# Head blocks 512 columns wide in a seven-phase transformer kernel, with MLA's mask, constants and two weight splits moved

## The chip, the cores and the metric

The kernel runs on one core of a Trainium2 chip. The time is device microseconds of one execution, and what counts is the median of several. TensorE (PE) multiplies matrices, VectorE (DVE) and ScalarE (ACT) work on elements, GpSimd (POOL) does a few small powers here, and SyncE (SP) issues the DMAs. Matmuls write to PSUM, eight banks of 512 fp32 values a partition; the other engines take the results from there to SBUF.

## The reference

Everything is fp32, for 256 positions and a model width of 1024. Two blocks run one after the other; in the first, each of two layers is a mixer and an MLP, each closed by a layer norm on the residual sum.

```python
# first block: layer 0 mixes by a short convolution, layer 1 by multi-head latent attention (MLA)
x = layer_norm(ALPHA * x + mixer(x))
x = layer_norm(ALPHA * x + square(relu(x @ w1)) @ w2)        # w1 1024 x 4096
# second block
x = x + 0.5 * ((silu(h @ w_gate) * (h @ w_up)) @ w_down)     # h = rms_norm(x), w_gate 1024 x 2816
x = x + hybrid(rms_norm(x))                                  # w_in to z, xbc, dt, q, k, v; SSD and attention; w_out
x = x + 0.5 * swiglu(rms_norm(x)); return rms_norm(x)
# inside MLA, 8 heads, chunks of 64 positions
ckv, kpe = split(x @ w_dkv, 256);  ckv = rms_norm(ckv, g_kv);  kpe = rope(kpe)
cq = rms_norm(x @ w_dq, g_q);  q = cq @ w_uq                 # 128 + 64 (rope) a head
k, v = ckv @ w_uk, ckv @ w_uv
s = (q_nope @ k.T + q_pe @ kpe.T) * scale
p = softmax(where(k_chunk <= q_chunk, s, -inf));  y = (p @ v) @ w_o
```

## The kernel before

Seven phases follow each other: sc (short convolution), mlp0, mla, mlp1, ffn1, hyb and ffn2. TensorE keeps fp32 accuracy by splitting each operand into a high and a low part: a product is three matmuls, high times high, high times low weight, low activation times high weight (`mmx`, L176 to L178).

All weights go through one stream. A list, the plan, names the tiles in the order in which they are used, mostly 512 KB each (128 partitions of 1024 values). SP's queue loads a tile into one of four raw buffers; ScalarE casts it to the high part (L156), VectorE subtracts that from the raw tile for the low part (L157); eleven such pairs can be in SBUF. `take(n, ahead)` hands out the next n pairs and starts the splits of those behind them, `rel` gives pairs back. SP's instructions run in the order in which the program writes them. On the other engines a scheduler sets the order, with a higher priority for the end of a phase (`fin`).

The positions are two halves of 128, hh = 0 and 1. A phase ends with the accumulators of half 0, whose norm then runs on VectorE beside the matmuls of half 1. The next phase begins with "head" blocks: `xblock` holds a 128 x 128 piece of the transposed activations in the array and streams 256 weight columns, 8 pieces of the contraction, for half 0; `flush_norm` then transposes the normalised rows of half 1, and the same weights are used for that half. mlp0 and mlp1 have four such blocks in front (`m`), ffn1 and ffn2 two of the gate and two of the up weights (`pg`, `pu`), hyb four of v and z and later two more of z (`vz`). The weights of these blocks lie in HBM as 4 KB a partition for 256 columns and four contraction pieces. What follows a head streams 512 columns, of activations in the wide blocks (`wd`) and of weights in the output blocks (`acc`).

MLA has no such head; its first matmuls are `pkv` (w_dkv, 320 columns) and `pq` (w_dq, 384 columns), again for half 0 and then half 1. `chain_kv` normalises a half's ckv (`ch`) and turns its kpe (`rope`, results in `kp`); both are transposed later (`tp<-ident,ch` and `tp<-ident,kp`). g_q, g_kv and the rope's table are loaded into three work buffers at the start of MLA. Behind the two halves stands the line that starts the splits of w_uv, w_uk and w_uq:

```python
wuv, wuk, wuq = self.take(2, 0), self.take(2, 0), self.take(6, 0)
```

`scores` writes four heads, or two for the 256 keys of half 1, into a bank `sc`: a matmul with k, one with kpe, and a third that adds the mask as the product of a row of ones for the first 64 queries and a row of a large negative number for the last 64 keys (`mr`, bf16). `soft` takes the maximum, the exponentials (ScalarE, one for each head) and the sum, and multiplies by its reciprocal (`pp<-pp,rc`). The eight heads go in two groups of four; between them stand a v projection, the k projections and the q projections of the second group, whose results VectorE copies out (`qT`, L776).

Of the kernel before, what the change touches and what calls it, by code (L numbers as in the profile page):

```python
# [16 lines left out]
P = 128  # L17
D = 1024
S = 256
# [15 lines left out]
WORK_BUFS = 37  # L35
# [51 lines left out]
class Core:  # L87
# [48 lines left out]

    def dma_ahead(self):
        while self.n_dma < len(self.plan) and self.n_dma < self.n_split + RAW_BUFS:
            src, nk, nn = self.plan[self.n_dma]
            r = self.rawp.tile([P, SUB], F32, tag="raw", name="raw")  # L140
            self.nc.sync.dma_start(out=r[:, :nk * nn].rearrange("p (k n) -> p k n", k=nk), in_=src)
            self.raw[self.n_dma] = r
            self.n_dma += 1

    def pump(self, n=99):

        nc = self.nc
        self.dma_ahead()
        while n > 0 and self.n_split < len(self.plan) and self.n_split < self.n_rel + W_BUFS:
            i = self.n_split  # L150
            _, nk, nn = self.plan[i]
# [6 lines left out]
            self.wt[i] = (h[:, :m].rearrange("p (k n) -> p k n", k=nk), l[:, :m].rearrange("p (k n) -> p k n", k=nk))  # L158
            self.n_split += 1
            self.dma_ahead()  # L160
            n -= 1
# [123 lines left out]
    def layer_norm(self, hh, acc, g, b):  # L285
# [119 lines left out]
    def sc(self, fin):  # L405
# [4 lines left out]
        for b in range(4):  # L410
# [22 lines left out]
            if b == 0:  # L433
                self.constants()
        self.tail(self.new_acc(), [(vT, k) for k in range(8)], True, fin, 4)

    def constants(self):
# [18 lines left out]
        nc.vector.tensor_scalar(out=self.ones, in0=self.tri, scalar1=0.0, scalar2=1.0, op0=ALU.mult, op1=ALU.add)  # L456

# [63 lines left out]
    def plan_mlp(self, i):  # L521
        w1, w2 = self.t["ff_w1"][2 * i:2 * i + 2], self.t["ff_w2"][i]
        f = {"a": lambda j: self.wi(w1, j * S), "b": lambda j: [self.wap(w2, 2 * j + k, 1, 0, D) for k in range(2)]}
        nb = D_FF // S
        o = ([("a", j) for j in range(self.HEAD)] + self.mlp_order(nb, self.HEAD, self.TAIL)
             + [("b", j) for j in range(nb - self.TAIL, nb)])
        return [x for c, j in o for x in f[c](j)]
# [28 lines left out]
    def mlp(self, fin):  # L556
# [4 lines left out]
        for hh in range(2):  # L561
            for j in range(self.HEAD):
# [4 lines left out]
                self.xblock(ps[:, (j % 2) * S:(j % 2 + 1) * S], xT, hh, ws[j])  # L567
# [28 lines left out]
    def plan_ffn(self, i):  # L596
# [4 lines left out]
        o = ([("a", j) for j in range(self.HEAD2)] + self.mlp_order(nb, self.HEAD2, self.TAIL2)  # L601
             + [("b", j) for j in range(nb - self.TAIL2, nb)])
        return [x for c, j in o for x in f[c](j)]

    def ffn(self, fin):
# [60 lines left out]
    def mla(self, fin):  # L666
        nc, xT = self.nc, self.xT
        gq, gkv = self.work(name="gq")[:, :384], self.work(name="gkv")[:, :256]
        nc.sync.dma_start(out=gq, in_=self.t["mla_g_q"][0].partition_broadcast(P))
        nc.sync.dma_start(out=gkv, in_=self.t["mla_g_kv"][0].partition_broadcast(P))  # L670
        rt = self.work(name="rope")[:, :256].rearrange("p (h c r) -> p h c r", h=2, c=2)
# [3 lines left out]
        mr = self.const.tile([1, 3, S], BF16, tag="mr", name="mr")  # L675
        nc.vector.memset(mr, 0.0)
        nc.vector.memset(mr[:, 0, 0:64], 1.0)
        nc.vector.memset(mr[:, 1, 64:128], NEG)
        nc.vector.memset(mr[:, 2, 192:256], NEG)
# [49 lines left out]
        wuv, wuk, wuq = self.take(2, 0), self.take(2, 0), self.take(6, 0)  # L729
# [50 lines left out]
        def scores(hh, heads):  # L780
            nk = P * (hh + 1)
            ps = self.ps("sc")
            for i, h in enumerate(heads):
# [5 lines left out]
                                 start=False, stop=False)  # L789
                nc.tensor.matmul(o, lhsT=mr[:, 0, :P], rhs=mr[:, 1 + hh, :nk], start=False, stop=True)  # L790
# [116 lines left out]
    def plan_hyb(self):  # L907
        wi = lambda o: self.wi(self.t["w_in_2"], o)
        p = wi(self.O_V) + wi(self.O_V + S) + wi(0) + wi(S)
        for b in (4, 5, 0, 1, 2, 3):  # L910
            p += wi(self.O_XBC + S * b)
        p += wi(2 * S) + wi(3 * S)
# [3 lines left out]
    def hyb(self, fin):  # L916
# [58 lines left out]
        for hh in range(2):  # L975
            ps = self.ps("vz")
            for i in range(2):
                self.xblock(ps[:, i * S:(i + 1) * S], xT, hh, ws[2 * i:2 * i + 2])
# [445 lines left out]
```

## Time and profile before

| | before |
|---|---|
| median of three runs | 1110.56 us (1106.35 to 1114.09) |
| profiled execution | 1109.88 us, its span 1108.0 us |
| TensorE busy | 1092.5 us, 99% of the span, 6278 matmuls |
| VectorE / ScalarE / GpSimd busy | 738.9 / 585.3 / 22.6 us |
| mean granted clock of TensorE | 0.996 |
| read from HBM | 197.79 MB, 179 GB/s over the span |

The span is what the profiler recorded from the first to the last instruction; the execution's own time is 1.9 us longer. The granted clock is a share of full speed, 2.4 GHz; half of it is the lower level of 1.2 GHz. In the slices of the page TensorE is at 9 tenths or more in nearly all, with one slice of 8 where MLA lies and a 7 at the end.

### The profile page before, as it was taken

What the parts mean: (1) busy time and instruction counts of PE and PEld (TensorE: products, weight loads), DVE (VectorE), ACT (ScalarE), POOL (GpSimd) and SP (SyncE); (2) the same over time, 40 slices, a digit from 0 to 9 for tenths busy, and PEclk for the clock granted to TensorE, in tenths of its full rate; (3) what the DMA queues carried; (4) which work ended last, traced back from release to release, by engine and by line L of the source; (5) the groups of instructions that cost most, each with busy time, mean ns of one, the idle gap of its engine ahead of it and who ended that gap; (6) DMA issues with size and microseconds to landing.
All of it is one profiled execution on the core that took longest, in us unless ns stands there. A gap on an engine that the chain in (4) does not pass through costs nothing. (4 is left out here: it accounts for less than half of the span.)

```text
span 1108.0 us, 16365 instructions
## 1 busy us (share of the span) xinstructions
PE 1092.5 (99%) x6278; PEld 957.7 (86%) x6278; DVE 738.9 (67%) x1174; ACT 585.3 (53%) x1005; POOL 22.6 (2%) x34
## 2 busy tenths in 40 slices
PE   8999999999999999999999999999999899999997
PEld 7888988888888998888898888889899689888886
DVE  6987656666856775666586656665988666665653
ACT  5764645453446374445355555555775465555541
POOL 0000000000100000000000000000000000000000
PEclk9999999999999999999999999999999999999999
DMA  7875666653634466666457666555653235655631
GB/s 260 265 256 161 223 191 189 192 189 119 206 131 171 136 207 190 191 190 191 166 193 234 191 190 191 188 182 188 189 199 96 76 133 197 219 193 190 189 116 38
DMA packets 60238, 199.90 MB, mean 180 GB/s; under 512 B 7168, under 2 KB 12032, under 8 KB 60160
## 3 DMA queue, kind: packets, MB, share of 16 engines
q1 hardware_dynamic: 60160, 198.86, 56.2%
q8 instruction: 49, 0.80, 0.3%
q14 instruction: 29, 0.24, 0.1%
HBM read 197.79 MB, written 1.05 MB: 179 GB/s over the span
## 5 line engine op out<-in xcount | busy, mean ns | idle before, releaser
L157 DVE TENSOR_TENSOR wl<-raw,wh 128x1024 fp32r<-128x1024 f32 (+2 forms) x360 | 433.7, 1212 | 178.5 <-ACT wh L156 99.8
L156 ACT CAST wh<-raw 128x1024 fp32r<-128x1024 f32 (+2 forms) x360 | 368.9, 1043 | 197.6 <-PE acc L178 84.3
L202 PE MATMUL wd<-fx,wh 128*128 128x512 f32 x1312 | 330.8, 394 | 0.0
L202 PEld LDWEIGHTS wd<-fx,wh 128*128 128x128 f32 x1312 | 239.0, 190 | 44.4 <-ACT wh L156 0.4
L176 PE MATMUL acc<-wh,fh 128*128 128x512 f32 (+1 forms) x544 | 214.2, 394 | 0.0
L177 PE MATMUL acc<-wl,fh 128*128 128x512 f32 (+1 forms) x544 | 212.3, 390 | 0.0
L178 PE MATMUL acc<-wh,fl 128*128 128x512 f32 (+1 forms) x544 | 211.3, 389 | 0.0
L204 PEld LDWEIGHTS wd<-fx,wl 128*128 128x128 f32 x1312 | 179.6, 191 | 12.9
L204 PE MATMUL wd<-fx,wl 128*128 128x256 f32 x1312 | 183.5, 283 | 0.0
L178 PEld LDWEIGHTS acc<-wh,fl 128*128 128x128 f32 x544 | 102.2, 188 | 21.2
L176 PEld LDWEIGHTS acc<-wh,fh 128*128 128x128 f32 x544 | 102.8, 189 | 20.2 <-issue 0.7
L177 PEld LDWEIGHTS acc<-wl,fh 128*128 128x128 f32 x544 | 102.8, 189 | 19.1
L205 ACT COPY gu<-wd 128x256 f32<-128x256 f32 x72 | 26.5, 368 | 64.4 <-PE wd L204 64.4
L206 DVE TENSOR_TENSOR gu<-wd,gu 128x256 f32<-128x256 f32 x72 | 30.3, 420 | 29.9 <-ACT gu L205 29.8
L229 ACT CAST fh<-r 128x512 fp32r<-128x512 f32 x24 | 14.9, 622 | 59.1 <-DVE r L584 59.1
L282 POOL TENSOR_TENSOR rstd<-rstd,nhalf 128x1 f32<-128x1 f32 x22 | 20.6, 935 | 978.3 <-DVE rstd L281 431.6
L176 PE MATMUL m<-wh,fx 128*128 128x256 f32 x128 | 36.8, 287 | 0.0
L247 DVE TENSOR_TENSOR fx<-tp,fx 128x128 fp32r<-128x128 f32 x112 | 23.7, 280 | 19.5 <-ACT fx L245 19.5
L178 PE MATMUL m<-wh,fx 128*128 128x256 f32 x128 | 36.5, 285 | 0.0
L177 PE MATMUL m<-wl,fx 128*128 128x256 f32 x128 | 36.3, 283 | 0.0
L229 ACT CAST fh<-gp 128x512 fp32r<-128x512 f32 x18 | 11.2, 621 | 43.8 <-DVE gp L614 43.8
L205 ACT COPY s<-wd 128x256 f32<-128x256 f32 x48 | 17.6, 367 | 27.0 <-PE wd L204 27.0
(273 smaller groups left out, 1216.7 us busy)
## 6 DMA issues: line engine op xcount, KB each, us to landing
raw<-in_ff_w_dram SPq DMA_DIRECT2D x128, 512.0 KB, 4.3
raw<-in_ffn_w_gate_dram SPq DMA_DIRECT2D x44, 512.0 KB, 4.3
raw<-in_ffn_w_up_dram SPq DMA_DIRECT2D x44, 512.0 KB, 4.3
raw<-in_ffn_w_down_dram SPq DMA_DIRECT2D x44, 512.0 KB, 4.1
raw<-in_w_in_dram SPq DMA_DIRECT2D x32, 512.0 KB, 4.3
raw<-in_sc_w_in_dram SPq DMA_DIRECT2D x23, 512.0 KB, 4.5
raw<-in_w_out_dram SPq DMA_DIRECT2D x12, 512.0 KB, 4.0
raw<-in_sc_w_out_dram SPq DMA_DIRECT2D x8, 512.0 KB, 4.7
```

The costliest lines, as they stand in the source:

```text
L156: nc.scalar.copy(h[:, :m], r[:, :m])
L157: nc.vector.tensor_tensor(out=l[:, :m], in0=r[:, :m], in1=h[:, :m].bitcast(F32), op=ALU.subtract)
L176: mm(out, lhsT=x[0], rhs=w[0], start=start, stop=False)
L177: mm(out, lhsT=x[0], rhs=w[1], start=False, stop=False)
L178: mm(out, lhsT=x[1], rhs=w[0], start=False, stop=stop)
L202: mm(ps, lhsT=w[0], rhs=xT.both(k), start=k == 0, stop=False)
L204: mm(ps[:, :S], lhsT=w[1], rhs=xT.full(k)[0], start=False, stop=k == len(parts) - 1)
L205: self.nc.scalar.copy(out, ps[:, S:])
L206: self.nc.vector.tensor_tensor(out=out, in0=ps[:, :S], in1=out, op=ALU.add)
L229: self.nc.scalar.copy(h, src)
L247: self.nc.vector.tensor_tensor(out=l, in0=src, in1=h.bitcast(F32), op=ALU.subtract)
L282: self.nc.gpsimd.tensor_tensor(out=r, in0=r, in1=self.nhalf, op=ALU.pow)
```

## The change

Four things are changed.

First, the head blocks stream 512 weight columns in one matmul. `wx` cuts the same 512 KB tiles differently: two neighbouring blocks of 256 columns and two contraction pieces, so a partition's part is two runs of 2 KB that lie apart in HBM. `xwide` uses two tiles a call, and its right operand is two runs of 256 columns, 512 apart, in each of the two parts of a pair. 44 tiles are loaded that way.

Second, MLA's mask is written by VectorE: after the two matmuls of each head a memset puts the negative number into the last 64 keys of the first 64 queries of all heads of the bank. The mask matmuls and `mr` with its memsets go.

Third, the VectorE part of the splits of w_uv and w_uk is held, in VectorE's order, behind the last instruction of the layer norm of half 1 that ends mlp0.

Fourth, MLA's three constants are loaded in the short conv's third block into a tile of their own, not at MLA's start; one work buffer fewer is reserved.

```diff
-WORK_BUFS = 37
+WORK_BUFS = 36
...
+    def wx(self, ap, n0):
+        two = [ap[k, n0 // S:n0 // S + 2].rearrange("b p (k n) -> p b k n", k=4) for k in range(2)]
+        return [(two[k // 2][:, :, 2 * (k % 2):2 * (k % 2) + 2], 2, 512, True) for k in range(4)]
...
+            if len(self.plan[i]) > 3:
+                self.wt[i] = tuple(a.rearrange("p (b k n) -> p k b n", b=2, k=nk) for a in (h, l))
...
+    def xwide(self, ps, xT, hh, ws, k0):
+        out = ps.rearrange("p (b n) -> p b n", b=2)
+        for i in range(4):
+            w = ws[i // 2]
+            self.mmx(out, xT.half(k0 + i, hh), (w[0][:, i % 2], w[1][:, i % 2]), k0 + i == 0, k0 + i == 7)
...
     def layer_norm(self, hh, acc, g, b):
...
+            last = nc.vector.scalar_tensor_tensor(out=x[:, s], in0=x[:, s], scalar=r, in1=b[:, s], op0=ALU.mult, op1=ALU.add)
+        self.norm_end = last.ins
...
     def sc(self, fin):
...
+            if b == 2:
+                self.mla_constants()
...
     def mlp(self, fin):
...
-                self.xblock(ps[:, (j % 2) * S:(j % 2 + 1) * S], xT, hh, ws[j])
+                self.xwide(ps, xT, hh, ws[j], 4 * (j % 2))
...
     def ffn(self, fin):
...
-                self.xblock((pg, pu)[i % 2][:, (i // 2) * S:(i // 2 + 1) * S], xT, hh, ws[i])
+                self.xwide((pg, pu)[i // 2], xT, hh, ws[i], 4 * (i % 2))
...
     def mla(self, fin):
-        nc.sync.dma_start(out=gq, in_=self.t["mla_g_q"][0].partition_broadcast(P))
-        nc.sync.dma_start(out=gkv, in_=self.t["mla_g_kv"][0].partition_broadcast(P))
...
-        nc.sync.dma_start(out=rt, in_=self.t["c_rope"].rearrange("(h p) c r -> p h c r", p=P))
+        norm_end = self.norm_end
+        gq, gkv, rt = self.mla_par
...
-        wuv, wuk, wuq = self.take(2, 0), self.take(2, 0), self.take(6, 0)
+        with self.tc.issue_after(norm_end):
+            wuv, wuk = self.take(2, 0), self.take(2, 0)
+        wuq = self.take(6, 0)
...
-                                 start=False, stop=False)
-                nc.tensor.matmul(o, lhsT=mr[:, 0, :P], rhs=mr[:, 1 + hh, :nk], start=False, stop=True)
+                                 start=False, stop=True)
+            nc.vector.memset(ps.rearrange("p (h k) -> p h k", k=nk)[:64, :, nk - 64:], NEG)
...
     def hyb(self, fin):
...
-                    self.xblock(ps[:, i * S:(i + 1) * S], xT, hh, ws[2 * o + i])
+                    self.xwide(ps, xT, hh, ws[2 * o + i], 4 * i)
```

How the instructions stand in a row at three places follows. `wl<-raw,wh` is the VectorE part of a split; 128x1024 at the start of MLA are the tiles of w_uv and w_uk, `x_87` the rows of half 1.

On VectorE at the start of MLA, before, from the split of the first w_uv tile to that of the last w_uk tile:

```order
L157 TENSOR_TENSOR wl<-raw,wh 128x1024
L290 SCALAR_TENSOR_TENSOR x_87<-x_87,acc_1456 128x512
L290 SCALAR_TENSOR_TENSOR x_87<-x_87,acc_1457 128x512
L291 BN_STATS bn<-x_87 128x6 x2
L157 TENSOR_TENSOR wl<-raw,wh 128x1024
L293 BN_AGGR mv<-bn 128x2
L157 TENSOR_TENSOR wl<-raw,wh 128x1024
L279 TENSOR_SCALAR rstd<-mv 128x1
L297 SCALAR_TENSOR_TENSOR x_87<-x_87,mv,gb 128x512 x2
L298 SCALAR_TENSOR_TENSOR x_87<-x_87,rstd,gb 128x512 x2
L279 TENSOR_SCALAR rstd<-ss 128x1
L157 TENSOR_TENSOR wl<-raw,wh 128x1024
```

After, the steps of the norm stand without a split between them; from the last of them to the copy into kp the order is:

```order
L316 SCALAR_TENSOR_TENSOR x_87<-x_87,rstd,gb 128x512 x2
L297 TENSOR_SCALAR rstd<-ss 128x1
L165 TENSOR_TENSOR wl<-raw,wh 128x1024
L714 SCALAR_TENSOR_TENSOR ch<-pkv,rstd,mlap 128x256
L691 TENSOR_TENSOR rm<-pkv,mlap 128x32
L692 TENSOR_TENSOR rm<-pkv,mlap 128x32
L693 TENSOR_TENSOR kp<-pkv,mlap 128x64
L165 TENSOR_TENSOR wl<-raw,wh 128x1024
L694 TENSOR_TENSOR kp<-kp,rm 128x64
L297 TENSOR_SCALAR rstd<-ss 128x1
L165 TENSOR_TENSOR wl<-raw,wh 128x1024
L720 COPY kp<-kp 128x64
```

The splits between and ahead of the norm's steps now stand behind its last one, three of them ahead of kp's copy, among the steps of ch and of the rope.

On TensorE in MLA, before, where the second half of x is transposed and pkv of that half begins:

```order
L255 MATMUL tp<-ident,x_87 128x128 x8
L176 MATMUL pkv<-wh,fx 128x320
L177 MATMUL pkv<-wl,fx 128x320
L255 MATMUL tp<-ident,ch 128x128 x2
L178 MATMUL pkv<-wh,fx 128x320
```

After:

```order
L273 MATMUL tp<-ident,x_87 128x128 x8
L187 MATMUL pkv<-wh,fx 128x320
L188 MATMUL pkv<-wl,fx 128x320
L273 MATMUL tp<-ident,ch 128x128 x2
L726 MATMUL tp<-ident,kp 128x128 x2
L189 MATMUL pkv<-wh,fx 128x320
```

The transposes of half 0's kp, which stood behind the last matmul of this pkv block, now stand behind its second.

On VectorE between the first group's softmax and the second group's scores, before, from the split behind the second bank's maximum to the second copy of qT (`pp` are the exponentials, `rc` the reciprocal sums):

```order
L157 TENSOR_TENSOR wl<-raw,wh 128x1024
L892 RECIPROCAL rc<-sums 128x2
L883 TENSOR_REDUCE mx<-sc 128x2
L797 TENSOR_TENSOR pp<-pp,rc 128x512
L885 TENSOR_SCALAR nb<-mx 128x2
L157 TENSOR_TENSOR wl<-raw,wh 128x1024 x2
L892 RECIPROCAL rc<-sums 128x2
L776 COPY qT<-qT 128x512
L797 TENSOR_TENSOR pp<-pp,rc 128x512
L157 TENSOR_TENSOR wl<-raw,wh 128x1024
L776 COPY qT<-qT 128x512
```

After, from the same place to the second group's first memset:

```order
L165 TENSOR_TENSOR wl<-raw,wh 128x1024 x2
L916 RECIPROCAL rc<-sums 128x2
L907 TENSOR_REDUCE mx<-sc 128x2
L821 TENSOR_TENSOR pp<-pp,rc 128x512
L909 TENSOR_SCALAR nb<-mx 128x2
L165 TENSOR_TENSOR wl<-raw,wh 128x1024
L916 RECIPROCAL rc<-sums 128x2
L165 TENSOR_TENSOR wl<-raw,wh 128x1024
L821 TENSOR_TENSOR pp<-pp,rc 128x512
L800 COPY qT<-qT 128x512 x2
L165 TENSOR_TENSOR wl<-raw,wh 128x1024 x2
L814 MEMSET sc 64x4x64
```

Ahead of the first qT copy there are now four splits in place of three and both of the last multiplications of `pp` in place of one; the two copies stand together.

## Rows read from the trace of the kernel before

**Rows 1.** The page, part 1: busy us, share of the span, instructions.

```profile
PE 1092.5 (99%) x6278; PEld 957.7 (86%) x6278; DVE 738.9 (67%) x1174; ACT 585.3 (53%) x1005; POOL 22.6 (2%) x34
```

**Rows 2.** Timeline of TensorE in the hybrid's second z block (start us, length us).

```profile
765.61 0.28 PE L176 MATMUL vz<-wh,fx 128*128 128x256 f32 x1
...
771.25 0.28 PE L178 MATMUL vz<-wh,fx 128*128 128x256 f32 x1
```

**Rows 3.** Timeline of TensorE in an output block of mlp0.

```profile
149.75 0.39 PE L176 MATMUL acc<-wh,fh 128*128 128x512 f32 x1
...
154.29 0.39 PE L178 MATMUL acc<-wh,fl 128*128 128x512 f32 x1
```

**Rows 4.** Timeline of TensorE in q_pe: 256 columns in four runs of 64.

```profile
307.06 0.28 PE L177 MATMUL qpe<-wl,fh 128*128 128x256 f32 x1
...
308.97 0.28 PE L178 MATMUL qpe<-wh,fl 128*128 128x256 f32 x1
```

**Rows 5.** Timeline of TensorE in the MLA scores; x2 is one fp32 matmul.

```profile
321.02 0.39 PE L786 MATMUL sc<-kT,qT 128*128 128x128 f32 x2
...
324.11 0.70 PE L786 MATMUL sc<-kT,qT 128*128 128x256 f32 x2
...
329.19 0.50 PE L176 MATMUL v<-wh,fh 128*128 128x512 f32 x1
...
337.88 0.60 PE L899 MATMUL tp<-ident,pp 128*128 128x128 f32 x4
...
345.78 0.60 PE L786 MATMUL sc<-kT,qT 128*128 128x256 f32 x2
346.21 0.59 PE L788 MATMUL sc<-kpeT,qpeT 128*128 128x256 f32 x2
```

**Rows 6.** Timeline of VectorE beside the MLA scores.

```profile
331.28 1.23 DVE L157 TENSOR_TENSOR wl<-raw,wh 128x1024 fp32r<-128x1024 f32 x1 [2.10 <-ACT wh L156]
...
336.10 0.67 DVE L776 COPY qT<-qT 128x512 f32<-128x512 f32 x1
```

**Rows 7.** Timeline of VectorE at the start of MLA.

```profile
279.03 0.31 DVE L682 MEMSET kp<- 128x128 f32 x2
...
283.50 1.28 DVE L290 SCALAR_TENSOR_TENSOR x<-x,acc 128x512 f32<-128x512 f32 x2
...
286.31 1.23 DVE L157 TENSOR_TENSOR wl<-raw,wh 128x1024 fp32r<-128x1024 f32 x1 [0.34 <-ACT wh L156]
...
290.13 1.41 DVE L298 SCALAR_TENSOR_TENSOR x<-x,rstd,gb 128x512 f32<-128x512 f32 x2
...
293.17 0.48 DVE L692 SCALAR_TENSOR_TENSOR ch<-pkv,rstd,gkv 128x256 f32<-128x256 f32 x1 [0.44 <-POOL rstd L282]
...
294.43 0.18 DVE L698 COPY kp<-kp 128x64 f32<-128x64 f32 x1
```

**Rows 8.** Timeline of TensorE in the same place.

```profile
282.17 0.31 PE L176 MATMUL pkv<-wh,fx 128*128 128x320 f32 x1
...
290.93 1.32 PE L255 MATMUL tp<-ident,x 128*128 128x128 f32 x8 [0.92 <-DVE x L298]
...
293.71 0.59 PE L255 MATMUL tp<-ident,ch 128*128 128x128 f32 x2 [1.17 <-DVE ch L692]
294.24 0.64 PE L178 MATMUL pkv<-wh,fx 128*128 128x320 f32 x1
...
298.93 0.38 PE L704 MATMUL tp<-ident,kp 128*128 128x128 f32 x2
```

**Rows 9.** Stretches: length, then PE, PEld, DVE, ACT, POOL busy, PEclk, DMA, GB/s.

```profile
295.00:297.00 2.00, 2.00 (x9) 2.00 (x9) 1.67 (x8) 0.45 (x1) 0.55 (x1) 0.50 0.12 46
297.00:299.00 2.00, 2.00 (x15) 2.00 (x14) 1.10 (x2) 1.13 (x2) 0.00 (x0) 0.93 0.00 0
```

**Rows 10.** DMA issues by line: count, KB each, median us to landing.

```profile
raw<-in_ff_w_dram SPq DMA_DIRECT2D x128, 512.0 KB, 4.3
...
raw<-in_mla_w_dkv_dram SPq DMA_DIRECT2D x2, 480.0 KB, 3.8
```

More of the change, by code (lines that the diff above doesn't have):

```diff
@@ L135, in wap @@
         return (ap[k0 * P:(k0 + nk) * P, n0:n0 + nn].rearrange("(k p) n -> p k n", p=P), nk, nn)
+    def wx(self, ap, n0):
+        two = [ap[k, n0 // S:n0 // S + 2].rearrange("b p (k n) -> p b k n", k=4) for k in range(2)]
+        return [(two[k // 2][:, :, 2 * (k % 2):2 * (k % 2) + 2], 2, 512, True) for k in range(4)]
     def dma_ahead(self):
         while self.n_dma < len(self.plan) and self.n_dma < self.n_split + RAW_BUFS:
-            src, nk, nn = self.plan[self.n_dma]
+            src, nk, nn = self.plan[self.n_dma][:3]
             r = self.rawp.tile([P, SUB], F32, tag="raw", name="raw")
-            self.nc.sync.dma_start(out=r[:, :nk * nn].rearrange("p (k n) -> p k n", k=nk), in_=src)
+            if len(self.plan[self.n_dma]) > 3:
+                self.nc.sync.dma_start(out=r.rearrange("p (b k n) -> p b k n", b=2, k=nk), in_=src)
+            else:
+                self.nc.sync.dma_start(out=r[:, :nk * nn].rearrange("p (k n) -> p k n", k=nk), in_=src)
             self.raw[self.n_dma] = r
@@ L150, in pump @@
             i = self.n_split
-            _, nk, nn = self.plan[i]
+            _, nk, nn = self.plan[i][:3]
             r = self.raw.pop(i)
@@ L456, in constants, with mla_constants @@
         nc.vector.tensor_scalar(out=self.ones, in0=self.tri, scalar1=0.0, scalar2=1.0, op0=ALU.mult, op1=ALU.add)
+    def mla_constants(self):
+        nc = self.nc
+        pt = self.const.tile([P, 896], F32, tag="mlap", name="mlap")
+        gq, gkv = pt[:, :384], pt[:, 384:640]
+        rt = pt[:, 640:].rearrange("p (h c r) -> p h c r", h=2, c=2)
+        nc.sync.dma_start(out=gq, in_=self.t["mla_g_q"][0].partition_broadcast(P))
+        nc.sync.dma_start(out=gkv, in_=self.t["mla_g_kv"][0].partition_broadcast(P))
+        nc.sync.dma_start(out=rt, in_=self.t["c_rope"].rearrange("(h p) c r -> p h c r", p=P))
+        self.mla_par = gq, gkv, rt
     def tail(self, acc, items, first, fin, flush_at):
@@ L524, in plan_mlp @@
         nb = D_FF // S
-        o = ([("a", j) for j in range(self.HEAD)] + self.mlp_order(nb, self.HEAD, self.TAIL)
-             + [("b", j) for j in range(nb - self.TAIL, nb)])
-        return [x for c, j in o for x in f[c](j)]
+        o = self.mlp_order(nb, self.HEAD, self.TAIL) + [("b", j) for j in range(nb - self.TAIL, nb)]
+        head = [x for j in range(0, self.HEAD, 2) for x in self.wx(w1, j * S)]
+        return head + [x for c, j in o for x in f[c](j)]
     def relu2(self, ps, n=512):
@@ L600, in plan_ffn @@
         f = {"a": lambda j: self.wi(g, j * S) + self.wi(u, j * S), "b": lambda j: [self.wap(d, 2 * j + k, 1, 0, D) for k in range(2)]}
-        o = ([("a", j) for j in range(self.HEAD2)] + self.mlp_order(nb, self.HEAD2, self.TAIL2)
-             + [("b", j) for j in range(nb - self.TAIL2, nb)])
-        return [x for c, j in o for x in f[c](j)]
+        o = self.mlp_order(nb, self.HEAD2, self.TAIL2) + [("b", j) for j in range(nb - self.TAIL2, nb)]
+        return self.wx(g, 0) + self.wx(u, 0) + [x for c, j in o for x in f[c](j)]
     def ffn(self, fin):
@@ L908, in plan_hyb @@
         wi = lambda o: self.wi(self.t["w_in_2"], o)
-        p = wi(self.O_V) + wi(self.O_V + S) + wi(0) + wi(S)
+        wx = lambda o: self.wx(self.t["w_in_2"], o)
+        p = wx(self.O_V) + wx(0)
         for b in (4, 5, 0, 1, 2, 3):
             p += wi(self.O_XBC + S * b)
-        p += wi(2 * S) + wi(3 * S)
+        p += wx(2 * S)
         p += wi(self.O_Q) + wi(self.O_Q + S) + wi(self.O_K) + wi(self.O_K + S)
@@ L977, in hyb @@
             for i in range(2):
-                self.xblock(ps[:, i * S:(i + 1) * S], xT, hh, ws[2 * i:2 * i + 2])
+                self.xwide(ps, xT, hh, ws[2 * i:2 * i + 2], 4 * i)
                 if hh == 1:
```

11 lines of the change are left out of this document (2 added, 9 removed).

## The prediction

> **What bounds the kernel now.** I read the page's busy shares first: TensorE works 1092.5 of 1108.0 us [rows 1], so the waits together hold no more than about 15 us, and the question for each edit is what it does to TensorE's own time and to its few waits. A matmul's length is a poor measure of its price, since consecutive ones overlap: in the hybrid's second z block one of 256 columns is .28 long, but 47 steps lie between the starts at 765.61 and 771.25, .120 us each [rows 2]. So I went through timelines and took the distance from start to start. In an output block of mlp0, 20 steps of 512 columns take 4.54, .227 each [rows 3]. Then I read TensorE's and VectorE's timelines side by side in MLA, where TensorE waits, the clock there by stretches, and last the DMA issues.
>
> **Part 1: heads in 512 columns.** A head block is 8 parts of the contraction times 3 matmuls, for each half of the positions: 48 matmuls of 256 columns. Four blocks in each of mlp0, mlp1, ffn1 and ffn2 and six in the hybrid make 22 x 48 = 1056. They become 528 of 512 columns. A pair costs 2 x .120 = .240 now and .227 if the new shape runs at the pitch of rows 3: 528 x .013 = 6.9 us. The wide weight is read as two runs of 256 columns that lie apart; q_pe reads its weight in four runs of 64, and its 16 steps take 1.91, .119 each [rows 4], no more than unbroken columns. So the broken reading costs nothing. The two pitches are means that round: at .230 it would be 528 x .010 = 5.3. In ffn1 the transposes of the second half already wait for their normalised rows, so what the 48 pairs ahead of them save, .6, is waited away. I take 6.9 - .6 = **6.3**.
>
> The tiles stay as many and as large, but each partition reads two pieces of 2 KB where it read one of 4 KB. The nearest row to short pieces is w_dkv: 480 KB in rows of 1280 B land in 3.8 us, ff_w's 512 KB in 4.3 [rows 10]. I take nothing; the bad end is the last rival. MLA's three constants are issued on SP's queue in the short conv, behind a whole lookahead of weight tiles, and no longer ahead of MLA's weights. That brings w_uv and w_uk forward, whose splits now wait for the layer norm anyway: nothing. Their room comes from one work buffer, of which they held three: nothing.
>
> **Part 2: the mask.** For a group of four heads, scores over 128 keys take 321.02 to 324.11, 3.09, and over 256 keys 324.11 to 329.19, 5.08, with two fp32 matmuls and one mask matmul a head. One fp32 matmul over 256 keys takes 345.78 to 346.21, .43 [rows 5], and half of that over 128. Without the mask four heads cost 8 x .22 = 1.76 and 8 x .43 = 3.44: 1.33 + 1.64 = 2.97 saved a group, 5.9 for the two.
>
> VectorE must let that through. The memsets of the old mask's rows leave MLA's start, where nothing waited for them; three memsets a group come to it. No row shows one in PSUM. For the one of 256 elements the bounds are .155, half of two memsets of 128 elements in SBUF [rows 7], and .67, a copy of 512 elements out of PSUM [rows 6]; I take .3, nearer to a memset, and .2 for each of the two of 128 elements: .7 a group. The Trainium skill (PSUM — Partial Sum Buffer, Specifications (TRN2)) gives a VectorE memset 1.04 ns an element there, by estimate .53 a group; no run here shows it yet.
>
> Ahead of the second group's scores VectorE copies qT out. That copy starts at 336.10 and takes .67, and VectorE was idle for 2.10 until 331.28, waiting for a cast that waits for TensorE's v projection [rows 6]. In the changed order one more split (1.23), one more multiplication by rc (512 elements, .67 like the copy) and the memsets (.7) come before it: 2.6 more. Against that the projection comes 2.97 sooner and the idle time goes, so the copy ends between 336.0 and 337.3. TensorE is through its transposes 2.97 earlier, at 337.88 + .44 - 2.97 = 335.35 [rows 5], and waits until about 336.85: **1.5** lost. It then waits for transposed probabilities, behind four exponentials of ScalarE that follow it more closely; I put **1.0** on that, about the price of one more split in its way. Of 5.9 so **3.4** are left, between 1 (each wait over a microsecond longer) and 5.9 (none).
>
> **Part 3: the splits behind layer norm.** The second half's norm could start at 282.17, when TensorE has left the accumulators for pkv [rows 8]. It starts at 283.50, behind a split, ends at 291.54, and has two more splits of 1.23 inside [rows 7]: 8.04 - 2 x 1.23 = 5.6 of its own. With the splits behind it, it runs 282.2 to 287.8. But the splits are not gone. rstd's power on GpSimd takes 293.17 - 291.54 = 1.6 to come back, uv0's split runs beside it, and then ch (.48), the rope's steps, uv1, uk0 and the copy into kp follow. From ch to that copy's end it took 294.61 - 293.17 = 1.44 [rows 7]; with the two splits in between, 3.9. Two subtractions of transposed features, some .4, no longer stand there. So kp is ready near 287.8 + 1.6 + 3.9 - .4 = 292.9. That matters, because TensorE's new order has the kp transposes behind the second matmul of pkv, where they used to stand behind the last one. TensorE waited .92 for x and 1.17 for ch, and took up the rest of pkv at 294.24 [rows 8]; it will take it up near 293.1, after two transposes, **1.1** sooner.
>
> The clock adds to this. After those waits the granted clock is .50 (the level of 1.2 GHz) from 295 to 297, in which TensorE does 9 matmuls, and .93 from 297 to 299, in which it does 15 [rows 9]. The 22 matmuls from 294.24 to 298.93 [rows 8] took 4.69; at the second pace they take 22 x 2.00 / 15 = 2.9, which is 1.8 less. TensorE will still stand still there, in one long wait instead of two, so I take a fall that comes but ends sooner, .8 of the 1.8: **1.9** in all, between 0 (one wait for another) and 2.9.
>
> **The sum.** 6.3 + 3.4 + 1.9 = 11.6 from the profiled execution's 1109.88 gives 1098.3. The median of the runs is .7 higher, less than their distances from each other (about 4 us to either side); I write **1098.5**. About 1%, to 1099.45, is what a measurement of this kernel can tell from no change.
>
> **Rivals.**
> *VectorE lets it through* (.18). The casts come forward by all of the 2.97, qT is there when TensorE wants it, and the clock hardly falls in MLA: 6.9 + 5.9 + 2.7 = 15.5, 1094.4. For it speaks VectorE's idle 2.10 [rows 6], against it the 2.6 of work put ahead of the copy.
>
> *MLA gives it back* (.20). The clock falls in spite of all, kp is as late as ch was, and the second group of scores waits for qT nearly as long as its mask took: the heads' 6.3 and 1 remain, 1102.6. For it speaks that VectorE has the same splits to do as before, in the one place where TensorE waits for it.
>
> *Wide matmuls gain nothing* (.06). If each run of a broken weight pays what a matmul of 256 columns pays, 512 columns cost .240 and the heads stay as they are: 3.4 + 1.9 = 5.3, 1104.6. Against it stand q_pe's four runs at .119 [rows 4]. The Trainium skill (TensorE: Matmul & The Clock Gate, Back-to-back issue gap) gives a matmul its columns at 2.4 GHz and 2.5 ns on top, so that a pair would save 2.5 ns: 1.3 us in all, 1103.3 by estimate. The trace disagrees so far: by that rule 256 and 512 columns take .109 and .216, the rows show .120 and .227, 11 ns more in both.
>
> *Short pieces slow the loads* (.06), the slower side. If the queues work by pieces and not by bytes, a tile in twice as many takes 2 x 4.3 = 8.6 us to land, and with four raw buffers in flight one comes every 2.15. A head's first pass takes 96 x .120 = 11.5 and eats 8 tiles, 1.44 each, so it would run short by 8 x .71 = 5.7 us, five times over: 28, less the 11.6, and less some 2 for tiles already split: 1124. It decides from a landing time of 4 x 1.44 = 5.8 us. Against it: w_dkv's shorter rows land in 3.8 [rows 10].
>
> **How the numbers follow.** The forecast has .50 and some 3 us of its own to either side. The range takes in the first three rivals and the bounds of the unknown costs, 15.7 off at best (1094.2) and 5.3 - .6 + 1 = 5.7 at worst (1104.2), with 2 us for the spread of the runs: 1092 to 1106. Only the slower side lies outside. Faster by over 1%: .31 of the forecast's .50, as 1098.5 lies so near the bound, .17 of the first rival and .03 of the second, .51. Slower .05, nearly all of the last rival. The rest, .44, is within 1%.
>
> **What the next profile would show.** Right: matmuls of the heads .227 apart; scores of 1.76 and 3.44 with no mask between; TensorE waiting about 1.5 for qT; the second norm at 5.6 and pkv's rest taken up near 293.1, less what mlp0's head saved. Wrong: .24 in the heads, TensorE waiting for DMA in a head, a wait of over 2.5 in the scores, a norm that ends as late as before. What would overturn the whole sum is a wait that I hold to be hidden in mlp1, the hybrid or ffn2: I put their slack at 3, 3 and 1.4 us from the timelines, and the first pass of their heads gets shorter by only 48 x .013 = .6.

## The result and the profile after

| | before | after |
|---|---|---|
| median | 1110.09 us, 4 runs (1106.35 to 1114.09) | 1095.69 us, 4 runs (1095.38 to 1098.86) |
| profiled execution | 1109.88 us, span 1108.0 | 1095.52 us, span 1093.4 |
| ratio of the times | | .9876, 95% interval .9837 to .9915 |

The kernel is 1.2% faster, 14.4 us by the medians. The page of the changed kernel, part 1 (the busy time of the engines):

```profile
PE 1077.4 (99%) x5734; PEld 924.4 (85%) x5734; DVE 738.3 (68%) x1176; ACT 584.8 (53%) x1005; POOL 24.8 (2%) x34
```

TensorE's busy time fell by 15.1 us against [rows 1] and its matmuls by 544: 528 in the heads, 16 of the mask. VectorE has the same work as before, and the mean granted clock is .999 in place of .996. So the span, 14.6 shorter, moved with TensorE, and the question is in which stages. The same stages cut from TensorE's timelines of the two profiled executions, each from the start of its first matmul to the start of the next stage's first:

| stage (us) | before | after | difference |
|---|---|---|---|
| heads: mlp0 / mlp1 | 25.59 / 25.59 | 24.39 / 24.41 | -1.20 / -1.18 |
| heads: ffn1 / ffn2 | 25.23 / 24.32 | 24.64 / 23.15 | -.59 / -1.17 |
| heads: hyb, first four blocks / the two z blocks later | 26.04 / 11.52 | 24.84 / 10.91 | -1.20 / -.61 |
| start of MLA, first pkv to the transposes of half 0's second ch | 16.98 | 13.77 | -3.21 |
| MLA from the first scores to the first output product | 29.01 | 25.21 | -3.80 |
| hyb, from the first transposes of vz to the second | 7.55 | 6.36 | -1.19 |
| lead-in to mlp0, all other stages together | | | -.4 |

The heads give 5.95, MLA 7.0, and 1.2 came from a place in hyb that the change does not touch.

**The heads.** TensorE's timeline of mlp0's head in the changed kernel, the first two matmuls of half 0 and the transposes behind its last:

```profile
100.98 0.39 PE L187 MATMUL m<-wh,fx 128*128 128x512 f32 x1
101.21 0.39 PE L188 MATMUL m<-wl,fx 128*128 128x512 f32 x1
...
111.86 1.03 PE L273 MATMUL tp<-ident,x 128*128 128x128 f32 x8
```

The first pass is 48 matmuls of 512 columns from 100.98 to 111.86: 10.88, .227 each, the pitch of [rows 3]. The 96 matmuls of 256 columns before took 11.51. The DMA issues by line in the changed kernel (count, KB, median us to landing) show the tiles of the heads among those of the same weights:

```profile
raw<-in_ff_w_dram SPq DMA_DIRECT2D x128, 512.0 KB, 4.3
raw<-in_ffn_w_gate_dram SPq DMA_DIRECT2D x44, 512.0 KB, 4.4
...
raw<-in_w_in_dram SPq DMA_DIRECT2D x32, 512.0 KB, 4.2
...
raw<-in_mla_w_uv_dram SPq DMA_DIRECT2D x2, 512.0 KB, 4.7
raw<-in_mla_w_uk_dram SPq DMA_DIRECT2D x2, 512.0 KB, 4.5
```

The weights that hold the 2 KB pieces land in 4.2 to 4.4, against 4.3 in [rows 10]. These are medians over all tiles of a weight, and the heads' tiles are a part of them: mlp0's eight by themselves land in 3.6 to 4.6, against 3.5 to 4.6 before, mlp1's in 3.5 to 8.6, against 3.5 to 9.2. TensorE waits for no load in any head. w_uv and w_uk, behind no constants now, land in 4.7 and 4.5, against 6.2 and 6.8 before.

**The start of MLA.** VectorE's timeline in the changed kernel, the norm's first and last step, two of the splits behind it and the copy into kp:

```profile
280.34 1.37 DVE L308 SCALAR_TENSOR_TENSOR x<-x,acc 128x512 f32<-128x512 f32 x2 [1.53 <-PE acc L189]
...
284.57 1.41 DVE L316 SCALAR_TENSOR_TENSOR x<-x,rstd,gb 128x512 f32<-128x512 f32 x2
...
288.35 1.22 DVE L165 TENSOR_TENSOR wl<-raw,wh 128x1024 fp32r<-128x1024 f32 x1
...
289.68 1.21 DVE L165 TENSOR_TENSOR wl<-raw,wh 128x1024 fp32r<-128x1024 f32 x1
290.81 0.19 DVE L720 COPY kp<-kp 128x64 f32<-128x64 f32 x1
```

The norm starts at 280.34 and its last step ends at 285.98, 5.64, where it took 8.04 in [rows 7]. Three splits stand behind it, two of them between the rope's steps (288.35 and 289.68). TensorE's timeline there:

```profile
288.50 1.04 PE L273 MATMUL tp<-ident,x 128*128 128x128 f32 x8
...
291.06 0.33 PE L726 MATMUL tp<-ident,kp 128*128 128x128 f32 x1 [0.68 <-DVE kp L720]
291.25 0.41 PE L189 MATMUL pkv<-wh,fx 128*128 128x320 f32 x1
...
294.59 0.49 PE L273 MATMUL tp<-ident,ch 128*128 128x128 f32 x3
```

TensorE no longer waits for x (the transposes at 288.50 have no idle time ahead) or ch. What is left is .68 for kp, behind VectorE's splits at 288.35 and 289.68. And the granted clock by stretches (columns as in [rows 9]):

```profile
293.00:295.00 2.00, 2.00 (x16) 1.99 (x16) 2.00 (x4) 1.69 (x4) 0.00 (x0) 1.00 0.42 154
```

It is 1.00 there and in the stretches before. So the 22 matmuls of pkv's rest, from 291.25 to 294.59, took 3.34 in place of 4.69.

**The scores.** TensorE's timeline in the changed kernel:

```profile
316.38 0.39 PE L810 MATMUL sc<-kT,qT 128*128 128x128 f32 x2
...
318.16 0.60 PE L810 MATMUL sc<-kT,qT 128*128 128x256 f32 x2
...
321.43 0.59 PE L187 MATMUL v<-wh,fh 128*128 128x512 f32 x1
...
331.93 0.46 PE L810 MATMUL sc<-kT,qT 128*128 128x128 f32 x2 [1.14 <-DVE qT L800]
...
339.77 2.05 PE L839 MATMUL oT<-pT,vt 128*128 128x128 f32 x16 [0.59 <-ACT pT L925]
```

and VectorE's beside it:

```profile
319.14 0.27 DVE L814 MEMSET sc<- 64x256 f32 x1
...
320.56 0.17 DVE L814 MEMSET sc<- 64x128 f32 x1
...
330.50 0.69 DVE L821 TENSOR_TENSOR pp<-pp,rc 128x512 f32<-128x512 f32 x1
331.10 1.28 DVE L800 COPY qT<-qT 128x512 f32<-128x512 f32 x2
```

The scores of the first group take 1.78 and 3.27 (316.38 to 318.16 to 321.43) where [rows 5] show 3.09 and 5.08. TensorE then waits 1.14 for qT, whose two copies start at 331.10 behind a multiplication, and .59 at 339.77 for transposed probabilities. The memsets take .27 and .17.

### The profile page after: what moved, and what is told of

It reads as the page before. It is cut to its first block, busy times and chain, and to the rows that moved or that the text cites. A ratio compares the mean times of both kernels' runs of the same rounds, so it can differ in the third digit from the quotient of the medians.

```text
span 1093.4 us, 15275 instructions
## 1 busy us (share of the span) xinstructions
PE 1077.4 (99%) x5734; PEld 924.4 (85%) x5734; DVE 738.3 (68%) x1176; ACT 584.8 (53%) x1005; POOL 24.8 (2%) x34
## 5 line engine op out<-in xcount | busy, mean ns | idle before, releaser
L300 POOL TENSOR_TENSOR rstd<-rstd,nhalf 128x1 f32<-128x1 f32 x22 | 22.8, 1036 | 964.3 <-DVE rstd L299 429.4
L308 DVE SCALAR_TENSOR_TENSOR x<-x,acc 128x512 f32<-128x512 f32 x16 | 10.8, 686 | 28.8 <-PE acc L189 28.8
L263 ACT CAST fx<-tp 128x128 fp32r<-128x128 f32 x112 | 20.5, 300 | 16.5 <-PE tp L273 16.4
L217 DVE TENSOR_TENSOR s<-wd,s 128x256 f32<-128x256 f32 x48 | 20.1, 420 | 12.8 <-ACT s L216 12.8
```

The costliest lines, as they stand in the source:

```text
L217: self.nc.vector.tensor_tensor(out=out, in0=ps[:, :S], in1=out, op=ALU.add)
L300: self.nc.gpsimd.tensor_tensor(out=r, in0=r, in1=self.nhalf, op=ALU.pow)
```

## The experiments

Each was run beside the kernel before, on the same chip as it. For each the stages of the table above were cut again; one execution of each was profiled.

**Single parts, and the whole without the hold.** Four kernels: the heads alone; the mask alone; the hold of the splits alone, with the constants still loaded at MLA's start; the changed kernel without the hold.

For heads_only and mask_only the diff is the part of the change's own diff: `wx`, `xwide` and their calls in the one, the memset for the mask matmul in the other. In splits_only the kernel before gets

```diff
-        wuv, wuk, wuq = self.take(2, 0), self.take(2, 0), self.take(6, 0)
+        with self.tc.issue_after(norm_end):
+            wuv, wuk = self.take(2, 0), self.take(2, 0)
+        wuq = self.take(6, 0)
```

and in no_hold the changed kernel loses the same three lines again.

Expected, in this order:

> Only the wide heads; mask, constants and splits as before. The parts add up: each of the five heads and the second z block gets shorter as in the changed kernel (mlp0 and mlp1 1.2 each, ffn1 .6, hyb 1.8 in three places, ffn2 1.2), 6.0 us in all, about 1104 us. The start of MLA, from the first pkv matmul of half 0 to the transposes of half 0's last ch, stays at 17.0 with a granted clock near .50 behind TensorE's two waits. Rival, the clock falls by chance of the moment and not because of the waits: the same stretch comes out near 15.6 here. Rival, part of the gain came with other parts of the change: the heads give under 5.

> Only the mask written by VectorE; heads, constants and splits as before. The parts add up: from the first score matmul to the first output matmul of MLA 37.7 us in place of 41.5, TensorE waiting over 1 us for qT before the second group's scores, about 1106.3 us in all. Rival, VectorE's order there was made by the other parts: no wait for qT, and 36 us or less. The start of MLA as in the kernel before, 17.0, if the waits make the clock fall; near 15.6 if chance does.

> Only the splits of w_uv and w_uk held behind the layer norm; the constants are still loaded at the start of MLA, heads and mask as before. The hold does it: the norm of half 1 takes 5.6, TensorE does not wait for x, the clock stays at 1.0 and the start of MLA takes 13.8 in place of 17.0, about 1106.9 us in all. Rival, the earlier constants did it: with gq, gkv and the rope's table ahead of w_uv and w_uk on SP's queue the casts come late and the start takes 16 or more.

> The changed kernel without the hold: wide heads, mask by memset and early constants, the splits wherever the scheduler puts them. The hold does it: two splits stand inside the norm again, it takes about 8, TensorE waits for x and ch and the clock falls, the start of MLA takes 17 and the whole 1098.9. Rival, the earlier constants did it: the start takes 14 and the whole stays at 1095.7.

A fifth kernel has the early constants alone, `mla_constants` as in the change; it gives up two work buffers, one more than the change:

```diff
-WORK_BUFS = 37
+WORK_BUFS = 35
...
+            if b == 2:
+                self.mla_constants()
...
-        nc.sync.dma_start(out=gq, in_=self.t["mla_g_q"][0].partition_broadcast(P))
```

> Only MLA's constants loaded in the short conv (with one more work buffer given up for their room); heads, mask and splits as before. If the casts of w_uv and w_uk come late because of the constants' loads, VectorE no longer stands still inside the norm of half 1, and the start of MLA takes about 14.6 as without the hold; 17.0, 18.2 and 19.6 were seen with the late loads. Whole about 1107. Rival, the hold and the constants only work together with the heads: the start stays at 17 or more and the whole at 1109.8.

Measured (median us, its ratio to the kernel before, the stages that the parts touch in the profiled execution):

| kernel | median | ratio, 95% interval | heads, sum | start of MLA | scores |
|---|---|---|---|---|---|
| before | 1109.75 | | 138.29 | 16.98 | 29.01 |
| heads_only | 1104.15 | .9946 (.9924 to .9968) | 132.34 | 18.18 | 29.01 |
| mask_only | 1105.53 | .9957 (.9941 to .9974) | 138.28 | 19.62 | 25.09 |
| splits_only | 1107.81 | .9985 (.9967 to 1.0002) | 138.28 | 14.72 | 29.01 |
| consts_only | 1106.57 | .9973 (.9958 to .9987) | 138.26 | 14.86 | 29.01 |
| no_hold | 1097.58 | .9881 (.9856 to .9907) | 132.32 | 14.64 | 25.46 |
| after | 1095.69 | .9876 (.9837 to .9915) | 132.34 | 13.77 | 25.21 |

The heads and the mask came out as expected: 5.95 and 3.9 in the stages, 5.6 and 4.2 in the medians. The start of MLA did not: neither of my two theories of it stands. The hold alone takes it to 14.72, the early constants alone to 14.86 and 14.64, and only both to 13.77. Four views of heads_only, whose constants are loaded late: the DMA issues, a cast on ScalarE, a split on VectorE, and the transposes of x on TensorE:

```profile
raw<-in_mla_w_uk_dram SPq DMA_DIRECT2D x2, 512.0 KB, 8.9
...
gq<-in_mla_g_q_dram SPq DMA_DIRECT2D x1, 192.0 KB, 6.9
gkv<-in_mla_g_kv_dram SPq DMA_DIRECT2D x1, 128.0 KB, 8.6
```

```profile
284.12 1.05 ACT L164 CAST wh<-raw 128x1024 fp32r<-128x1024 f32 x1 [5.00 <-DMA raw<-in_mla_w_uv_dram]
```

```profile
285.20 1.23 DVE L165 TENSOR_TENSOR wl<-raw,wh 128x1024 fp32r<-128x1024 f32 x1 [2.44 <-ACT wh L164]
```

```profile
289.78 1.31 PE L273 MATMUL tp<-ident,x 128*128 128x128 f32 x8 [2.39 <-DVE x L316]
```

The constants' loads take 6.9 and 8.6 us, far more than their 192 and 128 KB would suggest beside 512 KB in 4.3, and w_uk's tiles behind them on SP's queue 8.9. ScalarE stands idle for 5.00 until w_uv's second tile is there. VectorE has that tile's split between two steps of the norm: it stands still for 2.44 there, and TensorE for 2.39 behind it. In the kernel before the same split waited .34 [rows 7]. In no_hold, with the loads early, three splits stand inside the norm and none waits:

```profile
281.02 1.22 DVE L165 TENSOR_TENSOR wl<-raw,wh 128x1024 fp32r<-128x1024 f32 x1
...
283.34 1.22 DVE L165 TENSOR_TENSOR wl<-raw,wh 128x1024 fp32r<-128x1024 f32 x1
...
285.08 1.21 DVE L165 TENSOR_TENSOR wl<-raw,wh 128x1024 fp32r<-128x1024 f32 x1
```

TensorE waits .86 for x and .26 for ch there:

```profile
288.63 1.32 PE L273 MATMUL tp<-ident,x 128*128 128x128 f32 x8 [0.86 <-DVE x L316]
...
290.50 0.44 PE L273 MATMUL tp<-ident,ch 128*128 128x128 f32 x2 [0.26 <-DVE ch L714]
```

In splits_only, with the loads late, the norm is short, but a cast on ScalarE waits 3.74 for the load, the squares for ch stand behind that cast, VectorE waits .87 for the squares, and TensorE waits .44 and .97 at kp's transposes (ScalarE's row, VectorE's, then TensorE's):

```profile
284.62 1.06 ACT L156 CAST wh<-raw 128x1024 fp32r<-128x1024 f32 x1 [3.74 <-DMA raw<-in_mla_w_uv_dram]
```

```profile
287.35 0.15 DVE L279 TENSOR_SCALAR rstd<-ss 128x1 f32<-128x1 f32 x1 [0.87 <-ACT ch L692]
```

```profile
291.20 0.33 PE L706 MATMUL tp<-ident,kp 128*128 128x128 f32 x1 [0.44 <-DVE rstd L279]
292.50 0.33 PE L706 MATMUL tp<-ident,kp 128*128 128x128 f32 x1 [0.97 <-DVE kp L700]
```

The same stage cut at two of TensorE's steps, each counted from the first pkv matmul (what is left to the stage's end holds kp's two transposes, .22, in the upper five):

| kernel (us) | x's transposes | pkv's rest taken up | from there to the end | granted clock there |
|---|---|---|---|---|
| before | 8.76 | 12.07 | 4.91 | falls to .50 |
| heads_only | 10.23 | 13.54 | 4.64 | falls to .50 |
| mask_only | 10.28 | 13.59 | 6.03 | falls to .50 |
| consts_only | 8.92 | 11.31 | 3.55 | 1.00 |
| no_hold | 8.71 | 11.10 | 3.54 | 1.00 |
| splits_only | 7.68 | 11.39 | 3.33 | 1.00 |
| after | 7.68 | 10.43 | 3.34 | 1.00 |

So there is more than one cause. VectorE's waits for late loads, in the norm and ahead of it, make x 1.5 later in heads_only and mask_only than in the kernel before. But that is not what consts_only gains on the kernel before: x comes no sooner there, and TensorE waits 1.08 for it. What comes .9 sooner behind x is ch. GpSimd's small power for its rstd takes 1.46 in the kernel before, beside the split that is left behind the norm, and .55 in consts_only, where all four splits are done by then and VectorE stands idle (GpSimd's row in each, then TensorE's in consts_only):

```profile
291.68 1.46 POOL L282 TENSOR_TENSOR rstd<-rstd,nhalf 128x1 f32<-128x1 f32 x1 [1.72 <-DVE rstd L279]
```

```profile
290.56 0.55 POOL L282 TENSOR_TENSOR rstd<-rstd,nhalf 128x1 f32<-128x1 f32 x1 [1.72 <-DVE rstd L279]
```

```profile
289.81 1.32 PE L255 MATMUL tp<-ident,x 128*128 128x128 f32 x8 [1.08 <-DVE x L298]
```

With the hold x is there in time, and a late load then counts through the squares on ScalarE: splits_only takes up pkv's rest .96 later than the changed kernel. The clock adds to all of this. In before, heads_only and mask_only TensorE's two waits make 2.1, 3.6 and 3.6 us, and the granted clock fell to .50 in or behind the second; in the other four of the table they make .7 to 1.4, and it stayed at 1.00, worth 1.36 between before and consts_only.

**The changed kernel once more.**

> The changed kernel once more, for what differs between two executions of it. If the clock behind TensorE's 2.6 us wait in hyb goes by the moment, the stretch from the first transposes of vz to the second takes either 6.4 or 7.6 here; the start of MLA, where the waits are under 1 us, stays at 13.8 with the clock at 1.0. Rival, the change set the clock there: 6.4 again. Whole 1095.7 to 1097.

The median was 1095.97 (1095.57 to 1100.9), the ratio .988 (.986 to .9899). The profiled execution was its longest, 1100.9. The start of MLA took 13.76, the heads what they took. But hyb's stretch behind its long wait took 9.82, neither of the two values expected, and the stage behind it 1.0 more. The clock by stretches there, in the kernel before, then in the changed kernel, then in this repeat:

```profile
864.00:866.00 2.00, 2.00 (x7) 1.81 (x8) 1.67 (x4) 1.29 (x4) 0.55 (x1) 0.50 0.55 217
```

```profile
852.00:854.00 2.00, 2.00 (x15) 1.45 (x14) 1.67 (x4) 1.17 (x4) 0.43 (x1) 1.00 0.42 164
```

```profile
855.00:857.00 2.00, 2.00 (x13) 1.77 (x13) 0.88 (x3) 0.00 (x0) 0.00 (x0) 0.50 0.00 0
```

TensorE stands idle for 2.42 ahead of this stretch in all thirteen profiles of this study (the 2.6 us wait of the expectation). It is here, at 859 to 886 us, that the page of the kernel before has its slice of 8, and not in MLA. The clock fell behind the wait in nine, the kernel before among them, and the stretch took 7.4 to 7.7 in eight of these and 9.82 in this one. It did not fall in four, the first profile of the changed kernel, mask_only, splits_only and hold_fx, with 6.36. In the repeat it stays at .50 from 853.9 to 863.9 us, in the kernel before from 863.9 to 867.2. Two executions of one kernel differ by 3.5 us here. So the 1.2 that the table shows for hyb belongs to the execution and not to the change. Why it falls in one and not in the other no run here tells.

**Can the last waits go?** Five versions of the changed kernel move what TensorE still waits for.

qt_act copies qT on ScalarE. hold_kp, hold_fx and hold_wo change what splits are held behind: those of w_uv and w_uk behind half 0's copy into kp, or behind the last low part of half 1's transposed x; six of w_o's behind the second group's qT. hold_both is hold_fx and hold_wo.

```diff
-                nc.vector.tensor_copy(qT[i], ps)
+                nc.scalar.copy(qT[i], ps)
```

```diff
-        with self.tc.issue_after(norm_end):
+        with self.tc.issue_after(kp_end[0]):
```

```diff
-        with self.tc.issue_after(norm_end):
+        with self.tc.issue_after(fx_end):
```

```diff
-        self.pump(2)
+        with self.tc.issue_after(self.qt_end):
+            self.pump(2)
...
-        ws = self.take(8, 0)
+        with self.tc.issue_after(self.qt_end):
+            ws = self.take(8, 0)
```

> The changed kernel with the qT copies on ScalarE instead of VectorE. TensorE waits for qT because the copy queues behind splits and a multiplication on VectorE: on ScalarE it follows the k copies at once, and the wait of 1.1 us before the second group falls to about .6; the scores' stretch takes 24.7 in place of 25.2. Rival, the q projection itself or another input of the scores is late: the wait stays at 1.1. Whole 1095.2.

> The changed kernel with the splits of w_uv and w_uk held behind the copy into kp of half 0, not behind the norm. TensorE waits .7 for kp behind two of the splits: without them the wait goes and the start of MLA takes 13.0 in place of 13.8, whole 1095.0. Rival, the delayed splits make TensorE wait for w_uv later: the start of MLA gains, and the stretch from there to the scores, 21.8, loses as much or more.

> The changed kernel with the splits of w_uv and w_uk held behind the last low part of half 1's transposed x. Behind kp's copy alone they only moved TensorE's wait from kp to the low parts of x (1.2 us). Behind both, TensorE waits for neither: the start of MLA takes 12.9 in place of 13.8, the rest as in the changed kernel, whole 1094.8. Rival, w_uv's parts are then late for the v projection: the stretch to the scores grows from 21.8 by as much.

> The changed kernel with six of w_o's eight splits held, in VectorE's order, behind the second group's qT copies. The wait of 1.1 us for qT is made by splits that VectorE does first and that nobody needs for another 20 us: it falls to .4 or less, and the scores' stretch takes 24.3 in place of 25.2. Rival, ScalarE's exponentials and copies set it, as the copy on ScalarE with its unchanged 1.1 could also mean: the wait stays over .9. Rival, the held splits come late for MLA's output: the stretch to mlp1's head, 26.8, grows.

> Both holds together. If each takes away its own wait, 12.9 and 24.3 stand together, 1.8 us less than the changed kernel, whole about 1094. Rival, what is held collects in front of the output product or of mlp1: the stretches behind give it back.

| kernel | median | ratio, 95% interval | start of MLA + projections up to the scores | scores |
|---|---|---|---|---|
| after, its repeat | 1095.69, 1095.97 | .9876, .9880 | 35.56, 35.55 | 25.21, 25.65 |
| qt_act | 1095.69 | .9874 (.9853 to .9894) | 35.52 | 25.41 |
| hold_kp | 1096.38 | .9884 (.9867 to .9902) | 36.03 | 25.10 |
| hold_fx | 1096.53 | .9879 (.9857 to .9902) | 37.78 | 25.09 |
| hold_wo | 1095.05 | .9867 (.9845 to .9889) | 35.53 | 25.88 |
| hold_both | 1096.76 | .9881 (.9860 to .9902) | 37.70 | 24.40 |

None is faster than the changed kernel by more than the intervals, and hold_kp, hold_fx and hold_wo gave back, in their profiles, what they took away. In qt_act the copy queues on ScalarE instead, behind exponentials and copies of v and kT, and TensorE's wait is still 1.09:

```profile
329.35 1.09 ACT L792 COPY kT<-kT 128x512 f32<-128x512 f32 x2
330.30 1.11 ACT L800 COPY qT<-qT 128x512 f32<-128x512 f32 x2
```

```profile
330.98 0.49 PE L810 MATMUL sc<-kT,qT 128*128 128x128 f32 x2 [1.09 <-ACT qT L800]
```

In hold_kp the copy into kp comes early (287.62), but three splits now stand ahead of the low parts of x, and TensorE waits 1.24 for those in place of .68 for kp:

```profile
287.73 2.35 DVE L165 TENSOR_TENSOR wl<-raw,wh 128x1024 fp32r<-128x1024 f32 x2
...
290.06 1.22 DVE L165 TENSOR_TENSOR wl<-raw,wh 128x1024 fp32r<-128x1024 f32 x1
291.19 1.67 DVE L265 TENSOR_TENSOR fx<-tp,fx 128x128 fp32r<-128x128 f32 x8
```

```profile
291.54 0.41 PE L189 MATMUL pkv<-wh,fx 128*128 128x320 f32 x1 [1.24 <-DVE fx L265]
```

In hold_fx both waits go, and the splits then meet q_pe: TensorE waits 1.53 for the rope of qpe, whose last step stands behind a split. The stages up to the scores take 2.2 longer, more than the rival said, and the place is q_pe and not the v projection.

```profile
309.81 0.66 PE L771 MATMUL tp<-ident,qpe 128*128 128x128 f32 x4 [1.53 <-DVE qpe L694]
```

In hold_wo the wait for qT goes altogether, as expected: VectorE's copy now waits for the q projection and nothing else (its row, then ScalarE's and TensorE's further on).

```profile
328.12 0.69 DVE L800 COPY qT<-qT 128x512 f32<-128x512 f32 x1 [0.23 <-PE qT L200]
```

```profile
336.67 1.05 ACT L164 CAST wh<-raw 128x1024 fp32r<-128x1024 f32 x1 [2.63 <-DMA raw<-in_mla_w_o_dram]
```

```profile
339.65 1.99 PE L839 MATMUL oT<-pT,vt 128*128 128x128 f32 x12 [1.96 <-ACT pT L927]
```

But TensorE comes to the product with v sooner and the transposed probabilities do not: the exponentials ahead of them stand on ScalarE behind a cast that waits 2.63 for a tile of w_o, late loads once more. The wait at the product grows from .59 to 1.96; the clock is .50 from 341 to 343 us, and MLA's output takes .95 longer.

In hold_both that second wait is 1.15, the clock stays up and the scores take 24.40, .1 from what was expected; hold_fx's loss outweighs it.

## Why the prediction was right

The forecast was 1098.5 and the measured median 1095.69; forecast and result are 11.6 and 14.4 us off the kernel before. Step by step:

- **The heads**, 6.3 forecast: 5.95. The pitch of .227 held, and the broken reading of the weight cost nothing: the pairs saved 13 ns each in mlp0's first pass, as forecast, which refutes the rival that wide matmuls gain nothing. The Trainium skill (TensorE: Matmul & The Clock Gate, Back-to-back issue gap) gives a matmul its columns at 2.4 GHz and 2.5 ns more, by which a pair saves 2.5 ns, 1.3 us in all by estimate; the trace disagrees, with 13 ns a pair. In ffn1 half of the saving was waited away as forecast, .59 being left of 1.2. The .35 too much is spread over the passes, which gave .63 and .57 in mlp0 and .61 in hyb's two z blocks: the saving of a pair is a difference of two rounded pitches, as the working said.
- **Short pieces**: nothing, as taken. mlp0's head tiles land in 3.6 to 4.6, under the 5.8 from which they would have decided; three of mlp1's take over 8, as two do in the kernel before, and TensorE waits for no load in a head. The slower side's rival is refuted.
- **The mask**, 3.4 forecast: 3.80. TensorE's own saving was 5.8 from start to start (5.9 forecast). It was held up twice, as forecast: 1.14 for qT (forecast 1.5) and .59 (forecast 1.0). The memsets took .27 and .17 (forecast .3 and .2). The Trainium skill (PSUM — Partial Sum Buffer, Specifications (TRN2)) gives a VectorE memset there 1.04 ns an element, timed with 2-byte elements: by estimate .27 for the first, as its row in the trace shows, and .13 for the second, whose row shows .17.
- **The splits behind layer norm**, 1.9 forecast: 3.21, the term that was mis-sized; 2.26 of it is the hold's own (splits_only), .95 that of the constants. The norm took 5.64 (forecast 5.6). It began at 280.34, which is 281.69 in the time of before (TensorE came to pkv 1.35 sooner), and not at 282.2: its first step needs only the first of the two accumulators. So kp was ready at 292.35 of that time, against 292.9 forecast, and pkv's rest was taken up 1.64 sooner and not 1.1. Without the early constants it was .68 (splits_only), less than forecast. And the clock did not fall at all: 1.35 in place of the .8 I took. The 1.8 that I gave it at most was misread: the 15 matmuls of [rows 9] are all that touch those two microseconds, and at a clock of 1.00 the 22 took 3.34 and not 2.9. The last .22 are kp's two transposes, which stand ahead of pkv's rest now.
- **The constants**, forecast at nothing: here the working failed, though the sum hardly shows it. I wrote that bringing w_uv and w_uk forward changes nothing, since their splits wait for the norm anyway. That looked at VectorE alone. With the hold, a late load still keeps a cast on ScalarE and ch's squares behind it: the hold without the early constants left .95 behind. Without the hold, consts_only took that stage from 17.0 to 14.86, by a shorter power on GpSimd and a clock that stayed up. I had also read the split inside the norm as 1.23 of work. It is a place where VectorE can wait for a load as well, .34 in the profile of before, and 2.44 in heads_only, where nothing was changed at this place. The profile I had showed a mild case.
- **Hyb**: 1.2 of the 14.6 between the two profiled executions is the clock's, behind a wait that both have. It was in no term and belongs in none.

The rival that MLA gives it all back (1102.6) is refuted by the two stages of MLA, 7.0 us shorter. The rival that VectorE lets everything through (1094.4) came near in time, for another reason: VectorE did hold TensorE up at both places of the scores, and the start of MLA gave the difference.

That the parts' gains add up is shown for the heads, whose stages make 132.31 to 132.35 in every kernel that has them, and within .6 for the mask, whose stage takes 25.09 alone and 25.21 and 25.65 in two executions of the changed kernel. For MLA's start it is shown that they do not. That the late constants also explain the wide scatter of the kernel before (1106.35 to 1115.73 over all its runs) is argued, not shown: one execution of it has a profile, and heads_only, with the same late loads, has eight of its nine runs within 1.5 us, which speaks against it.

## What to carry to other kernels

A cheap instruction placed inside a chain on an in-order engine costs its own time only if its data is there; before costing it, look at what it waits for in several executions, and at the loads ahead of that on the queue. Small broadcast loads held up the large ones behind them here, so constants belong where the lookahead is deep. When a part of a change gives time, look at which step came sooner before naming the cause: the early constants did not shorten the norm whose wait had pointed at them. And once TensorE is 99% busy and the engines beside it work in order, moving a burst of work moves the wait: five other placements of the same splits and copies gave other waits and no faster kernel.

## What the runs showed of the hardware

- Loads of 128 and 192 KB that spread one row over 128 partitions took 6.9 and 8.6 us to land at the start of MLA in heads_only, and the 512 KB tiles behind them on the queue 8.9; 6.8 to 8.9 in the four kernels with that order. With the constants elsewhere those tiles took 4.5 in the changed kernel and 4.2 in consts_only.
- The same 2.42 us wait of TensorE was followed by a fall of the granted clock to .50 in nine of thirteen profiles, at a cost of 1.0 to 1.4 us in eight of them and 3.5 in one, and by none in four; the changed kernel's two profiles are one of each.
- GpSimd's power of one value a partition took .55 us with VectorE idle, .89 to 1.00 when it began beside a step of the layer norm, 1.19 to 1.20 beside a split of 768 elements and 1.40 to 1.46 beside one of 1024, in all thirteen profiles and without an exception (69, 104, 14 and 81 of them).
- A right operand in two runs of 256 columns that lie 512 apart streamed at the pitch of 512 unbroken ones, .227 us.
- Dropping a bf16 matmul between fp32 ones saved more than an fp32 one of its width takes: four heads over 128 keys took 3.09 with it and 1.78 without, .33 a matmul, where a whole fp32 matmul over the same keys takes .22.
